# Attention: products with V issued in four groups of key tiles per block, TensorE in order of emission, one combination per query tile

## The chip, the cores and the metric

One core of a Trainium2 chip. The metric is the device time of one execution in microseconds (us), lower is better. Engines are named TensorE (PE), VectorE (DVE), ScalarE (ACT), GpSimd (POOL) and SyncE (SP, which issues the DMAs).

## The reference

A backbone of two layers over 256 context tokens and 2048 latent tokens, 1024 features. Each layer projects the normed stream, runs four branches side by side and projects their outputs back. The change lies in the branches A (differential attention) and B (grouped-query attention), which have four heads each, and are computed together, head by head:

```
# A: two softmax maps per head, q and k of 32 features, v of 64
s = jnp.einsum('bqhmd,bkhmd->bhmqk', q, k).astype(jnp.float32) * (DA_QK ** -0.5)
p = jax.nn.softmax(s, axis=-1)
w = p[:, :, 0] - lam * p[:, :, 1]
o = jnp.einsum('bhqk,bkhd->bqhd', w.astype(v.dtype), v)
# B: four query heads of 64 on two heads of k and v
s = jnp.einsum('bqhgd,bkhd->bhgqk', q, k).astype(jnp.float32) * (GQ_HD ** -0.5)
p = jax.nn.softmax(s, axis=-1)
return jnp.einsum('bhgqk,bkhd->bqhgd', p.astype(v.dtype), v)
```

Latent queries read all 2304 keys; context queries (in the first layer alone) read the 256 context keys.

## The kernel before

`attention` (line 743) runs once per layer, between the input projections and the output projection. It goes over the four heads, and within a head over eight **blocks** of 256 latent queries (two query tiles of 128), in the first layer with a small block of context queries ahead. That makes 32 full blocks a layer and 64 in all. A full block (`block`, line 825) has these steps:

- `da_chunk` (line 835), 12 times: for query tile qt, map m and one third of the keys (768), two TensorE matmuls of 384 columns write scores into a PSUM tile `s`; one VectorE scan (line 850) copies them to SBUF as `e` and keeps a running minimum of the negated scores.
- `da_exp` (line 856), 4 times: one ScalarE Exp over 2304 keys (line 858), with the sum of the row.
- `da_comb` (line 860), two parts per query tile: the two maps are combined, E0 + E1 r, where r comes from the sums (lines 865 and 866). The first 512 keys are done by ScalarE (line 871) and GpSimd (line 872), the other 1792 by VectorE in two instructions of 896 (line 875).
- `g_chunk` (line 880), 6 times: scores of B into a tile `s` of the same PSUM pool, and a VectorE scan (line 888) for their maximum alone. The pool `pf` has two such tiles, for `da_chunk` and `g_chunk` together.
- `qb` (line 894), twice: the maximum is transposed and written into the operand `qb`.
- `tr` (line 900), 9 times: four TensorE transposes (line 905) turn the combined map of two key tiles, and ScalarE copies them to SBUF as `wt` (line 909).
- `gs` (line 911), 9 times: scores of B, already turned (lines 917 and 918), their Exp by ScalarE as `gp` (line 920), and their sum over key tiles by GpSimd as `acc` (line 926).
- `pvm` (line 931), 18 times, one per key tile: the products with V. One matmul writes rows 64 to 127 of the PSUM tile `pv` (B, from `gp`), the other rows 0 to 63 (A, from `wt`); each uses half of the array's columns, and their records show them side by side. [...]
- `o1`, `o2`, `o3` (lines 942 to 970): `pv` is copied, transposed back, divided by the sums (four VectorE instructions at line 964) and stored.

The order comes from `Slots` (line 52): each step is put at a slot number with a priority, and the steps are traced in that order. The blocks overlap: a block's scores take its slots 0 to 17, its transposes, turned scores and products with V the 18 slots behind them, in which the next block's scores run. The lines that place the products are these:

```
S.at(b0 + 2 * u, lambda u=u: tr(u), 1)
S.at(b0 + 2 * u + 1, lambda u=u: gs(u), 4)
for j in range(2):
    S.at(b0 + 2 * u + 5.5 + j, lambda u=u, j=j: pvm(u, j), 5)
```

The traced program then goes through a scheduler, which sets the final order of each engine and may move an instruction ahead of others. Every engine executes its own list in that order.

Of the kernel before, what the change touches and what calls it, by code (L numbers as in the profile page):

```python
# [9 lines left out]
F32 = mybir.dt.float32  # L10
# [3 lines left out]
AF = mybir.ActivationFunctionType  # L14
# [6 lines left out]
P = 128  # L21
# [12 lines left out]
# columns of the input projection  # L34
# [6 lines left out]
def bc(ap, dims):  # L41
    """The access pattern with its free dimensions replaced (stride 0 repeats)."""
    return bass.AP(tensor=ap.tensor, offset=ap.offset, ap=[list(ap.ap[0])] + [list(d) for d in dims])


def rows_bc(ap, n):
    """A row of DRAM repeated over n partitions."""
# [4 lines left out]
class Slots:  # L52
    """Emission in the order of slots, so that blocks overlap."""
# [18 lines left out]
class Kernel:  # L72
# [3 lines left out]
    # ---------------------------------------------------------------- helpers  # L76
    def split_weights(self, wh, wl, src, w, col=None, stage=None):
        """wh + wl = src (scaled per row where col is given), both float32r."""
# [20 lines left out]
    def mm3(self, ps, hh, hl, wh, wl, c0, c1, ks=range(KT)):  # L99
        """ps = (hh + hl)^T (wh + wl) to float32's accuracy, over row tiles ks of KT."""  # L100
# [6 lines left out]
    def weights(self, wp, name, widths):  # L107
        """Tiles for the two parts of weights; the first are laid where a pool before frees its first."""
# [5 lines left out]
    def table(self):  # L114
        """The table set of Exp and Ln together."""
        return self.nc.scalar.preload_act_table_set("natural_log_exp_and_others")

    def rstd(self, pool, out, ss, n, tag, after=None):
        """out = (ss + n EPS)^(-1/2), with a step of Newton's on the engine's tables"""
# [17 lines left out]
    # ---------------------------------------------------------------- all  # L137
    def run(self):
        tc, nc, I = self.tc, self.nc, self.I
        self.table()  # L140
        with ExitStack() as cx:
# [6 lines left out]
            # per layer: (1 + sc) g and sh by feature, lambda  # L148
# [59 lines left out]
    # ---------------------------------------------------------------- modulation  # L208
    def ada(self, i, parts, wp, pp, start=False):
        """Shift (0), scale (1) and gate (2) of layer i, in steps of about a tile of weights."""  # L210
        nc, I = self.nc, self.I
        NB = 256
        if 2 in parts:
            # lambda, negated
# [11 lines left out]
        for r in parts:  # L226
# [33 lines left out]
            else:  # L260
                # rms_norm leaves out the factor 32 = sqrt(1024), which is put here
# [7 lines left out]
    # ---------------------------------------------------------------- q, k, v of A and B  # L269
    def rope(self, out, x, tmp, cos, sin, H, d):  # L270
        """out = x cos + swap(x) sin over H heads of d; x may lie in PSUM."""
# [20 lines left out]
    def pa_load(self, i, t):  # L292
        """Tile t of the stream, normed (but for gains), and its rotary factors."""
# [12 lines left out]
    def pa_front(self, i, t, xn, pt, tag):  # L306
        """Tile t modulated and transposed, in two float32r parts."""
# [19 lines left out]
    def h_tile(self, i, t):  # L327
        """The same, from memory."""
# [4 lines left out]
    def pa_weights(self, i):  # L333
        """Weights of q and k of A, and of q, k and v of B."""
# [8 lines left out]
    def proj_attn(self, i, X, H, wcx, W):  # L343
        nc, I, D = self.nc, self.I, self.D[i]
        last = i == DEPTH - 1
        with ExitStack() as cx:
# [29 lines left out]
            for t in range(NTILE):  # L376
# [10 lines left out]
                def part_a():  # L387
                    """A: q, k"""
# [950 lines left out]
```

## Time and profile before

| | |
|---|---|
| median of 3 runs | 4003.65 us (3995.14 to 4005.86) |
| span of the profiled execution, the one time that its page tells | 4001.6 us |
| TensorE busy | 3883.3 us, 97% |
| VectorE busy | 2730.4 us, 68% |
| ScalarE busy | 2322.1 us, 58% |
| GpSimd busy | 1461.5 us, 37% |
| attention, first layer, first to last score matmul | about 665 to 1601 us of the span |
| attention, second layer | about 2660 to 3567 us |

The shares of the page are means over the whole span. Attention is read by windows of its own: in the steady part of a layer one block follows the other at a fixed distance. Matmul records overlap, since matmuls are pipelined, so the distance between their starts tells more than their durations. In the chain of waits a run of equal matmuls is one row with its share of the time. On VectorE an instruction's record overlaps the next one's by some 0.08 us.

### The profile page before, as it was taken

To read this page: it belongs to the slowest core of one execution; us is meant where nothing else is said; L and a number is where in the kernel's file an instruction comes from. 1 tells how busy PE (TensorE), PEld (TensorE's weight loads), DVE (VectorE), ACT (ScalarE), POOL (GpSimd) and SP (SyncE) were. 2 spreads that over 40 slices of the span, in tenths; PEclk is the share of its full clock that TensorE was granted. 3 is DMA by queue.
4 is the path that set the end of the run, shared out by engine and by line. 5 is a ranking of instruction groups with operands and counts; after the bars stand their busy time and mean duration, and the time that the engine had idled before them with its cause. 6 is when DMAs were issued, how large, how long until landed. Compare 5 with 4: busy or idle time off the path is not lost.

```text
span 4001.6 us, 67227 instructions
## 1 busy us (share of the span) xinstructions
PE 3883.3 (97%) x24276; PEld 2877.1 (72%) x24276; DVE 2730.4 (68%) x6088; ACT 2322.1 (58%) x4181; POOL 1461.5 (37%) x1454
## 2 busy tenths in 40 slices
PE   7999998999999999999999999989999999999999
PEld 5888885666666666677878888866666666667777
DVE  5555545898989889533346654468999999976443
ACT  4434444677777777634444434447777777766554
POOL 1223221555555555311111132225555555552111
PEclk9999998999999999999999999979999999999999
DMA  8444334211020100533235431141111201015321
GB/s 265 148 150 133 115 99 111 65 41 43 22 67 21 33 24 24 182 103 104 94 120 179 143 119 56 60 106 49 45 34 29 56 21 31 22 50 169 103 95 58
DMA packets 302795, 339.21 MB, mean 85 GB/s; under 512 B 99384, under 2 KB 245760, under 8 KB 302464
## 3 DMA queue, kind: packets, MB, share of 16 engines
q1 hardware_dynamic: 302464, 334.92, 27.7%
q8 instruction: 192, 3.15, 0.3%
q14 instruction: 139, 1.14, 0.1%
HBM read 234.15 MB, written 100.62 MB: 84 GB/s over the span
## 4 chain that ended last, share of the span: by engine, by line
PE 87%; DMA 4%; DVE 4%; issue 2%; ACT 2%; POOL 1%; SPq 1%; DVEq 0%; POOLq 0%; ACTq 0%
PE pv L937 16%; PE s L845 8%; PE b L905 7%; PE b L917 5%; PE s L883 4%; PE b L918 3%; PE pz L103 3%; PE po L103 3%; PE po L105 3%; PE pz L105 3%; PE pz L104 3%; PE po L104 3%; PE pc L103 2%; PE pc L105 2%; PE pc L104 2%
## 5 line engine op out<-in xcount | busy, mean ns | idle before, releaser
L926 POOL TENSOR_TENSOR acc<-acc,gp 128x512 f32<-128x512 f32 x448 | 711.2, 1587 | 465.4 <-ACT gp L920 455.6
L937 PE MATMUL pv<-gp,v 128*64 128x256 f32 x2320 | 709.6, 400 | 0.0
L937 PE MATMUL pv<-wt,v 128*64 128x256 f32 x2320 | 709.2, 400 | 0.0
L858 ACT ACTIVATE e<-e,dm 128x2304 f32<-128x2304 f32 x256 | 568.7, 2221 | 48.3 <-DVE e L850 48.3
L850 DVE TENSOR_SCALAR_CACHE_REDUCE e<-s,dm 128x768 f32<-128x768 f32 x512 | 509.3, 1012 | 97.4 <-PE s L845 96.6
L845 PE MATMUL s<-dak,daq 128*128 128x384 f32 (+1 forms) x1568 | 461.8, 377 | 17.4 <-DMA daq<-aqk 7.4
L875 DVE SCALAR_TENSOR_TENSOR e<-e,r 128x896 f32<-128x896 f32 x256 | 457.8, 1808 | 0.1
L920 ACT ACTIVATE gp<-b 128x512 f32<-128x512 f32 x580 | 345.7, 596 | 100.5 <-PE b L918 87.9
L909 ACT COPY wt<-b 128x512 f32<-128x512 f32 x580 | 338.5, 585 | 112.5 <-PE b L905 99.0
L937 PEld LDWEIGHTS pv<-gp,v 128*64 128x64 f32 x2320 | 236.8, 135 | 205.8 <-issue 142.6
L905 PE MATMUL b<-ident,e 128*128 128x128 f32 x2304 | 360.7, 278 | 1.2 <-POOL e L872 1.2
L917 PE MATMUL b<-qa,ka 128*128 128x256 f32 x1160 | 354.2, 321 | 0.2
L905 PEld LDWEIGHTS b<-ident,e 128*128 128x128 f32 x2304 | 269.6, 141 | 93.7 <-issue 53.9
L845 PEld LDWEIGHTS s<-dak,daq 128*128 128x128 f32 x1568 | 247.7, 197 | 106.0 <-issue 85.5
L918 PE MATMUL b<-qb,kb 128*128 128x256 f32 x1160 | 305.5, 281 | 0.0
L917 PEld LDWEIGHTS b<-qa,ka 128*128 128x128 f32 x1160 | 220.7, 190 | 97.2 <-issue 71.6
L872 POOL TENSOR_TENSOR e<-e 128x512 f32<-128x512 f32 x128 | 171.2, 1337 | 306.5 <-ACT e L871 306.2
L888 DVE TENSOR_SCALAR_CACHE_REDUCE junk<-s,gm 128x768 bf16<-128x768 f32 x256 | 259.6, 1014 | 31.3 <-PE s L883 21.0
L850 DVE TENSOR_SCALAR_CACHE_REDUCE e<-s 128x768 f32<-128x768 f32 x256 | 239.6, 952 | 49.1 <-PE s L845 48.9
L1195 POOL TENSOR_TENSOR x<-x,g 128x512 f32<-128x512 f32 x66 | 88.8, 1345 | 427.1 <-DVE g L1193 406.4
L937 PEld LDWEIGHTS pv<-wt,v 128*64 128x64 f32 x2320 | 237.0, 135 | 0.6 <-issue 0.3
L883 PE MATMUL s<-ka,qa 128*128 128x384 f32 (+1 forms) x784 | 227.6, 373 | 9.1 <-DVE junk L888 6.2
(289 smaller groups left out, 9127.5 us busy)
## 6 DMA issues: line engine op xcount, KB each, us to landing
hT<-hT SPq DMA_DIRECT2D x104, 512.0 KB
dak<-aqk SPq DMA_DIRECT2D x96, 192.0 KB
daq<-aqk SPq DMA_DIRECT2D x136, 128.0 KB
wst<-in_w_in_dram SPq DMA_DIRECT2D x64, 256.0 KB
xa<-in_ada_w_dram SPq DMA_DIRECT2D x32, 512.0 KB
bst<-bst SPq DMA_DIRECT2D x68, 194.0 KB
xa<-xb SPq DMA_DIRECT2D x19, 512.0 KB
v<-v SPq DMA_DIRECT2D x16, 576.0 KB
```

Source lines behind the costliest of these rows:

```text
L845: nc.tensor.matmul(s[:, u, :hc], lhsT=Q["daq"][m][:, qt * P : (qt + 1) * P], rhs=R["dak"][m][c][:, u * hc : (u + 1) * hc], start=True, sto ...
L850: nc.vector.tensor_scalar(out=E[qt, m][:, c * ch : (c + 1) * ch].rearrange("p (u f) -> p u f", u=2), in0=s[:, :, :hc], scalar1=-SC, scalar ...
L858: nc.scalar.activation(e, e, AF.Exp, bias=NM[qt, m], scale=-1.0, accum_out=L[qt][:, m : m + 1])
L875: nc.vector.scalar_tensor_tensor(out=E0[:, a : a + w], in0=E1[:, a : a + w], scalar=RR[qt][:, 2:3], in1=E0[:, a : a + w], op0=ALU.mult, op ...
L883: nc.tensor.matmul(s[:, u, :hc], lhsT=Q["QA"][:, qt * P : (qt + 1) * P], rhs=R["KA"][c][:, u * hc : (u + 1) * hc], start=True, stop=True,)
L905: nc.tensor.transpose(s[:, j * 256 + qt * P : j * 256 + (qt + 1) * P], W[qt][:, k * P : (k + 1) * P], ident)
L909: nc.scalar.copy(WT[u], s)
L917: nc.tensor.matmul(o, lhsT=R["KA"][k // 6][:, ks], rhs=Q["QA"], start=True, stop=False)
L918: nc.tensor.matmul(o, lhsT=R["KB"][k // 6][:, ks], rhs=Q["QB"], start=False, stop=True)
L920: nc.scalar.activation(g, s, AF.Exp, scale=0.125)
L926: nc.gpsimd.tensor_tensor(out=B["acc"], in0=B["acc"], in1=g, op=ALU.add)
L937: nc.tensor.matmul(B["pv"][o : o + 64, :256], lhsT=R["V"][:, k, o : o + 64], rhs=x[:, js], start=k == 0, stop=k == nkt - 1,)
```

## The change

All of it lies in `attention`. The lines shift by three to five in the changed kernel.

```diff
+            cx.enter_context(self.tc.manual_schedule(engines={PE}))
...
                         if m == 0:
                             L[qt] = sp.tile([P, 2], F32, name="l", tag="l", bufs=6)
+                            if qt == 0:
+                                B["r"] = sp.tile([P, 2, 4], F32, name="r", tag="r", bufs=4)
...
-                        r = RR[qt] = sp.tile([P, 4], F32, name="r", tag="r", bufs=6)
-                        nc.vector.reciprocal(r[:, 0:2], l)
+                        r = RR[qt] = B["r"][:, qt]
+                        nc.vector.reciprocal(r[:, 0:3:2], l)
...
-                    rl = sp.tile([P, 4], F32, name="rl", tag="rl", bufs=3)
-                    nc.vector.reciprocal(rl, op[:, 256:260])
-                    B["op"], B["rl"] = op, rl
+                    nc.vector.reciprocal(B["r"][:, :, 1], op[:, 256:260:2])
+                    B["op"] = op
...
-                    for qt in range(2):
-                        for o, sc in ((0, RR[qt][:, 0:1]), (64, rl[:, 2 * qt : 2 * qt + 1])):
-                            dst, src = ob[:, qt, o : o + 64], op[:, qt * P + o : qt * P + o + 64]
-                            nc.vector.tensor_scalar(out=dst, in0=src, scalar1=sc, scalar2=None, op0=ALU.mult)
+                    nc.vector.tensor_tensor(
+                        out=ob.rearrange("p t (b d) -> p t b d", d=64),
+                        in0=B["op"][:, 0:256].rearrange("p (t b d) -> p t b d", t=2, d=64),
+                        in1=bc(B["r"][:, :, 0:2], [[4, 2], [1, 2], [0, 64]]), op=ALU.mult,
+                    )
...
-                    npt = 2 if full else 1
+                    npt = 1
...
-                    S.at(s, lambda qt=qt: qb(qt), 2)
+                    S.at(s + full, lambda qt=qt: qb(qt), 8 if full else 2)
...
-                        for j in range(2):
-                            S.at(b0 + 2 * u + 5.5 + j, lambda u=u, j=j: pvm(u, j), 5)
-                    e = b0 + 2 * (nu - 1) + 6.5
+                    for us in ((0, 1), (2, 3), (4, 5), (6, 7, 8)):
+                        for u in us:
+                            for j in range(2):
+                                S.at(b0 + 2 * us[-1] + 5.5, lambda u=u, j=j: pvm(u, j), 5)
+                    e = b0 + 2 * (nu - 1) + 5.5
```

So: TensorE's list in attention is the traced order, without the scheduler (`manual_schedule`). The 18 products with V of a block are traced in four runs, of 4, 4, 4 and 6. The VectorE part of a combination is one instruction of 1792 keys per query tile. The division at the end of a block is one instruction with the factors of both branches in one tile `r`. The transposes of `qb` come a slot later.

What TensorE has around a long run of products, in a steady block. Before (`s` are score tiles, `pv` the products with V, `b` with `e` the transposes, `b` with `qa` and `qb` the turned scores):

```order
L937 MATMUL pv<-gp,v 64x256
L937 MATMUL pv<-wt,v 64x256
L845 MATMUL s<-dak_32776,daq_33068 128x384 x2
L905 MATMUL b<-ident,e 128x128 x4
L845 MATMUL s<-dak_32779,daq_33066 128x384 x2
L937 MATMUL pv<-gp,v 64x256
L937 MATMUL pv<-wt,v 64x256
L917 MATMUL b<-qa,ka 128x256
L918 MATMUL b<-qb,kb 128x256
```

The run of six of the changed kernel, of whose twelve rows the first and the last two stand here:

```order
L909 MATMUL b<-ident,e 128x128 x4
L848 MATMUL s<-dak_32513,daq_32718 128x384 x2
L921 MATMUL b<-qa,ka 128x256
L922 MATMUL b<-qb,kb 128x256
L848 MATMUL s<-dak_32516,daq_32720 128x384 x2
L941 MATMUL pv<-gp,v 64x256
L941 MATMUL pv<-wt,v 64x256
...
L909 MATMUL b<-ident,e 128x128 x4
L848 MATMUL s<-dak_32432,daq_32718 128x384 x2
```

Products that stood singly between score tiles stand in one run, between the score tile of one slot and the transposes of the next. A steady block had 15 runs of products, and has 4; in the whole program they go from 976 to 264.

A run of four between score tiles of B (line 887), in the changed kernel, where again the first two of eight rows stand for the run:

```order
L887 MATMUL s<-ka,qa 128x384 x2
L921 MATMUL b<-qa,ka 128x256
L922 MATMUL b<-qb,kb 128x256
L941 MATMUL pv<-gp,v 64x256
L941 MATMUL pv<-wt,v 64x256
...
L887 MATMUL s<-ka,qa 128x384 x2
L909 MATMUL b<-ident,e 128x128 x4
```

Here a run lies between two score tiles, behind a pair of turned scores. The other two runs of four stand ahead of transposes: one right behind the transposes of `o2`, one behind the last score tile of B.

VectorE in a steady block before, from the division on (`ob`), with the scans of scores (`e`, `junk`) and the halves of the combination (L875):

```order
L964 TENSOR_SCALAR ob<-b,rl 128x64
L865 RECIPROCAL r<-l 128x2
L850 TENSOR_SCALAR e,dm<-s,dm 128x768
L866 SCALAR_TENSOR_TENSOR r<-l,nlam_70,r 128x1
L888 TENSOR_SCALAR junk,gm<-s 128x768
L875 SCALAR_TENSOR_TENSOR e<-e,r 128x896 x2
L888 TENSOR_SCALAR junk,gm<-s 128x768
L888 TENSOR_SCALAR junk,gm<-s,gm 128x768
```

The same place now:

```order
L958 RECIPROCAL r<-b 128x2
L879 SCALAR_TENSOR_TENSOR e<-e,r 128x1792
L963 TENSOR_TENSOR ob<-b,r 128x256
L853 TENSOR_SCALAR e,dm<-s,dm 128x768 x2
L892 TENSOR_SCALAR junk,gm<-s 128x768 x2
L892 TENSOR_SCALAR junk,gm<-s,gm 128x768 x2
L869 RECIPROCAL r<-l 128x2
```

One instruction of 1792 stands where two of 896 were, and two score tiles of A are queued behind it; the block's second combination stands behind the last scan of B.

## Rows read from the trace of the kernel before

**Rows 1.** The page's part 1: busy us, share of the span, instructions.

```profile
PE 3883.3 (97%) x24276; PEld 2877.1 (72%) x24276; DVE 2730.4 (68%) x6088; ACT 2322.1 (58%) x4181; POOL 1461.5 (37%) x1454
```

**Rows 2.** Windows, eight steady blocks: length, busy of PE, PEld, DVE, ACT, POOL, clock, DMA.

```profile
2902.80:3129.40 226.60, 225.72 (x1506) 150.97 (x1505) 205.82 (x392) 166.17 (x249) 127.90 (x89) 1.00 0.16 40
```

**Rows 3.** Waits in the same eight blocks: us in total, times, longest.

```profile
DVE e L850 <- PE s L845: 15.6, 40, 0.5
PEld b L896 <- PE pv L937: 4.3, 8, 0.5
DVE junk L888 <- PE s L883: 3.8, 16, 0.3
```

**Rows 4.** Chain of waits, two steady blocks: start, us, what, number of matmuls.

```profile
2909.38 0.58 PE pv L937 x4
2909.97 0.59 PE b L905 x4
...
2913.32 1.01 PE pv L937 x8
...
2917.34 1.47 PE pv L937 x12
...
2925.66 0.36 PE s L845 x2
2926.25 0.58 PE pv L937 x4
2926.83 0.56 PE s L845 x2
2927.39 0.44 PE b L905 x4
...
2941.65 1.01 PE pv L937 x8
```

**Rows 5.** Timeline of PE, four turned scores and the score tile behind them.

```profile
1202.65 0.28 PE L918 MATMUL b<-qb,kb 128*128 128x256 f32 x1
1202.77 0.29 PE L917 MATMUL b<-qa,ka 128*128 128x256 f32 x1
1202.89 0.28 PE L918 MATMUL b<-qb,kb 128*128 128x256 f32 x1
1203.01 0.51 PE L845 MATMUL s<-dak,daq 128*128 128x384 f32 x2
```

**Rows 6.** Timeline of DVE in one steady block.

```profile
2904.05 0.25 DVE L964 TENSOR_SCALAR ob<-b,r 128x64 f32<-128x64 f32 x1
2904.22 0.27 DVE L964 TENSOR_SCALAR ob<-b,rl 128x64 f32<-128x64 f32 x1
2904.41 0.28 DVE L964 TENSOR_SCALAR ob<-b,r 128x64 f32<-128x64 f32 x1
...
2907.13 4.26 DVE L875 SCALAR_TENSOR_TENSOR e<-e,r 128x896 f32<-128x896 f32 x2
...
2915.86 1.95 DVE L875 SCALAR_TENSOR_TENSOR e<-e,r 128x896 f32<-128x896 f32 x1
...
2918.68 1.22 DVE L875 SCALAR_TENSOR_TENSOR e<-e,r 128x896 f32<-128x896 f32 x1
...
2921.57 1.01 DVE L850 TENSOR_SCALAR_CACHE_REDUCE e<-s,dm 128x768 f32<-128x768 f32 x1
2922.51 0.08 DVE L850 DVE_READ_ACCUMULATOR e<-s,dm 128x1 f32 x1
2922.51 1.01 DVE L850 TENSOR_SCALAR_CACHE_REDUCE e<-s,dm 128x768 f32<-128x768 f32 x1
```

**Rows 7.** Timeline of POOL in the same block.

```profile
2907.07 1.29 POOL L872 TENSOR_TENSOR e<-e 128x512 f32<-128x512 f32 x1 [2.48 <-ACT e L871]
2908.32 5.57 POOL L926 TENSOR_TENSOR acc<-acc,gp 128x512 f32<-128x512 f32 x3
2915.59 1.27 POOL L872 TENSOR_TENSOR e<-e 128x512 f32<-128x512 f32 x1 [1.71 <-ACT e L871]
2916.83 2.12 POOL L926 TENSOR_TENSOR acc<-acc,gp 128x512 f32<-128x512 f32 x1
2920.51 1.29 POOL L926 TENSOR_TENSOR acc<-acc,gp 128x512 f32<-128x512 f32 x1 [1.57 <-ACT gp L920]
```

**Rows 8.** Groups by line and shape in the eight blocks, DVE: busy us, mean ns, idle before.

```profile
L875 DVE SCALAR_TENSOR_TENSOR e<-e,r 128x896 f32<-128x896 f32 x32 | 59.4, 1875 | 0.0
```

More of the change, by code (lines that the diff above doesn't have):

```diff
@@ L863, in da_comb @@
                     if part == 0:
-                        r = RR[qt] = sp.tile([P, 4], F32, name="r", tag="r", bufs=6)
-                        nc.vector.reciprocal(r[:, 0:2], l)
+                        r = RR[qt] = B["r"][:, qt]
+                        nc.vector.reciprocal(r[:, 0:3:2], l)
                         nc.vector.scalar_tensor_tensor(
-                            out=r[:, 2:3], in0=l[:, 0:1], scalar=nlam, in1=r[:, 1:2], op0=ALU.mult, op1=ALU.mult
+                            out=r[:, 3:4], in0=l[:, 0:1], scalar=nlam, in1=r[:, 2:3], op0=ALU.mult, op1=ALU.mult
                         )
@@ L870, in da_comb @@
                         if npl:
-                            nc.scalar.activation(E1[:, :npl], E1[:, :npl], AF.Copy, scale=r[:, 2:3])
+                            nc.scalar.activation(E1[:, :npl], E1[:, :npl], AF.Copy, scale=r[:, 3:4])
                             nc.gpsimd.tensor_tensor(out=E0[:, :npl], in0=E0[:, :npl], in1=E1[:, :npl], op=ALU.add)
@@ L875, in da_comb @@
                     nc.vector.scalar_tensor_tensor(
-                        out=E0[:, a : a + w], in0=E1[:, a : a + w], scalar=RR[qt][:, 2:3], in1=E0[:, a : a + w],
+                        out=E0[:, a : a + w], in0=E1[:, a : a + w], scalar=RR[qt][:, 3:4], in1=E0[:, a : a + w],
                         op0=ALU.mult, op1=ALU.add,
@@ L953, in o2 @@
                         )
-                    rl = sp.tile([P, 4], F32, name="rl", tag="rl", bufs=3)
-                    nc.vector.reciprocal(rl, op[:, 256:260])
-                    B["op"], B["rl"] = op, rl
+                    nc.vector.reciprocal(B["r"][:, :, 1], op[:, 256:260:2])
+                    B["op"] = op
                 def o3():
-                    op, rl = B["op"], B["rl"]
                     ob = sp.tile([P, 2, P], F32, name="ob", tag="ob", bufs=3)
-                    for qt in range(2):
-                        for o, sc in ((0, RR[qt][:, 0:1]), (64, rl[:, 2 * qt : 2 * qt + 1])):
-                            dst, src = ob[:, qt, o : o + 64], op[:, qt * P + o : qt * P + o + 64]
-                            nc.vector.tensor_scalar(out=dst, in0=src, scalar1=sc, scalar2=None, op0=ALU.mult)
+                    nc.vector.tensor_tensor(
[3 more added lines that the diff above has]
+                    )
                     for o in (0, 64):
```

## The prediction

> **What bounds the kernel now.** I read the shares first: TensorE is busy 97% of the span, VectorE 68% [rows 1]. That is a mean over stages, so I went to the windows of attention. Eight steady blocks take 226.60 us, 28.33 each; two equal runs of the chain, one block apart, stand 28.33 us apart as well (2913.32 and 2941.65) [rows 2, 4]. In them TensorE is busy 225.72 us (28.2 a block) at the full clock, VectorE 205.82 (25.73 a block), ScalarE 166.17, GpSimd 127.90 [rows 2]. So TensorE bounds the stage, and VectorE has only 2.6 us a block to spare. The waits agree: VectorE waits for score tiles, 15.6 and 3.8 us in eight blocks, never over 0.5 us at once, and TensorE's only wait of size is 0.5 us a block for the transposes of the maximum, most of it hidden behind the products' tail [rows 3].
>
> What does TensorE spend on the products with V? In the chain a run of one call (four records) has 0.58 us, of two 1.01, of three 1.47 [rows 4]. A further call costs 0.43 to 0.46, so the run itself costs 0.14. Its neighbours pay too: a score tile beside runs has 0.56 where one behind other work has 0.36, and the transposes behind a run have 0.59 instead of 0.44 [rows 4]. **A run costs 0.14 + 0.15 to 0.20, some 0.31 us, beside its products.** There are 15 runs in a steady block.
>
> **The change, part by part.**
>
> *Fewer runs.* 15 become 4: 11 x 0.31 = 3.4 us a block off TensorE. Its work falls from 28.2 to 24.8 us, under VectorE's 25.7. The 18 products themselves stay. So from here on TensorE alone no longer sets the block, and the question is what VectorE does, and how well the two fit.
>
> *The combination in one piece.* The four halves of a block took 2.13 twice (4.26 together), 1.95 and 1.22 us [rows 6], 59.4 / 8 = 7.43 a block [rows 8]. The same instruction is short when GpSimd is idle (1.22; GpSimd's add overlapped only its first 0.27 us) and nearly twice as long beside a GpSimd addition (2.13, under rows 2907.07 and 2908.32 of GpSimd) [rows 6, 7]. Per element that is 1.36 against 2.38 ns. One instruction of 1792 is therefore bounded by about 2.1 us (alone: two of 1.22, less the overlap and one start-up) and 4.26 (beside GpSimd throughout). GpSimd's own work is unchanged, 127.90 / 8 = 16.0 us a block [rows 2], and the 512 keys that it does itself start within 0.3 us of the VectorE part, with queued additions to `acc` behind them, up to 6.8 us on end [rows 7]. So I take 3.75 each, the mean of the halves before, nearest to the long end: 7.5 a block, no gain beyond one start-up.
>
> *The division.* Four instructions of 64 columns, 0.17 to 0.19 us from start to start [rows 6], become one of 256 that reads PSUM. Bounds: 0.19 (no more than one of 64) and 0.76 (all four). A scan of 768 columns from PSUM needs 0.94 [rows 6], so 256 come to about 0.4: 0.36 saved.
>
> *VectorE's work* is then 25.73 - 7.43 + 7.5 - 0.36 = 25.4 us a block.
>
> *VectorE's new waits.* TensorE may be ahead by two score tiles only (the pool `pf`), and executes its list in order. Around the run of six it goes: score tile, six products, four transposes, score tile. From one tile's end to the next's that is 0.58 + 5 x 0.445 = 2.80, then 0.59, then 0.36: 3.75 us [rows 4]. Meanwhile VectorE has the finished tile (0.94) and at most what is left of the one before: that one must have been begun when TensorE began the new tile, so at most 0.94 - 0.36 = 0.58. It idles 3.75 - 1.52 = 2.2 us at least, 2.8 at most: 2.4. Around the run of four between two tiles of B: turned scores 4 x 0.12 = 0.48 [rows 5], the run 0.58 + 3 x 0.445 = 1.92, a tile between runs 0.56: 2.96. Less 1.52 or 0.94: 1.4 to 2.0, taken as 1.6. The other two runs of four stand where VectorE is inside a combination (3.75 against 1.92 + 0.59), and cost it nothing. Idle in sum: 4.0 us a block (3.6 to 4.8).
>
> *Why it can't catch up.* Each combination holds both score tiles. The tile of TensorE's list that is third from its start waits for the combination, the division and a scan; from `o2` on TensorE has 1.92 + 0.59 + 0.36 + 0.48 + 0.36 = 3.7 us of work until then, VectorE needs 0.1 + 3.75 + 0.4 + 0.94 = 5.2. TensorE stalls about 1.5 us there, and likewise at the second combination, and whatever it saved on runs goes there. Before, the list let it do single products in these places.
>
> *The rest.* The transposes of `qb` a slot later remove the small wait [rows 3]; TensorE's stalls hide that, so 0. The tile `r` and the end `e` change no instruction on the path. SP issues the same loads and stores in each block, and TensorE's list outside attention is the same: 0.
>
> **Sum.** A block takes VectorE's work and idle time: 25.4 + 4.0 = 29.4 us, against 28.33: +1.07. TensorE's 24.8 plus its stalls fit in that. With 64 full blocks this is +68 us. The profiled span is 4001.6 us, and no time of that execution around it is told; the median of the runs is 4003.65, 2 us more. On the median: **4072 us**, 1.7% slower. Bounds: combinations of 3.3 with idle time of 3.6 give 24.5 + 3.6 = 28.1 (-15 us); of 4.26 with 4.2, 26.4 + 4.2 = 30.6 (+147, all at the bad end).
>
> **Rivals.** A difference under 0.3% (12 us, 0.19 us a block) is about what a measurement of this kernel can't tell from none.
>
> 1. *VectorE at its floor (faster).* If VectorE is fed without gaps, a block falls to its work, 25.4 us: 2.93 x 64 = 188 us less, 3816. Half of the idle time gone gives 27.4: 60 us less, 3944. It decides at 2.9 us of idle time a block; below that the kernel is faster. For it: TensorE's saving is real in every row of a run, and VectorE is 91% busy already. Against it: two score tiles hold 1.9 us of scans, and the run of six with its transposes lasts 3.4. The Trainium skill, TensorEngine Tiling (Array Packing), section PSUM Bottleneck, says that where the array is sped up by tiling, the copies out of PSUM may become the bound. By that rule alone the block would be the work of the emptying engine, which is this rival. No row before shows it: VectorE still waits for score tiles [rows 3]. Chance 0.24, mostly between 3925 and 3990.
>
> 2. *No difference.* The longer instruction meets less of GpSimd: combinations of 3.2 each make 24.3 of work, with 4.0 idle 28.3. For it: one of the four halves ran nearly alone [rows 6, 7]. Against it: a piece twice as long is less able to miss GpSimd's queue. 4004 us, chance 0.10.
>
> 3. *The order doesn't do what it says*, as where the list were still rearranged. The list of the changed program shows the four runs, so I count this with the second.
>
> **How the numbers follow.** The forecast (slower, VectorE and TensorE by turns waiting) has 0.66, the second rival 0.10, the first 0.24. Slower by over 0.3%: 0.66; within: 0.10; faster: 0.24. The slow case by itself runs from 4016 to 4120. For 8 in 10 the range must take in the slow case almost whole, the second rival and the near part of the first: 3925 to 4118.
>
> **What would show it.** After: (a) distance of two blocks 29.4 us; 28.33 or less refutes me. (b) TensorE's runs with 16 and 24 records, about 1.9 and 2.8 us, and its busy time near 25 us a block; if it stays at 28, the cost of a run was misread. (c) VectorE waiting for TensorE in pieces of over 1.4 us, twice a block, 3.6 to 4.8 us in sum. (d) TensorE waiting for the scans at lines 853 and 892, 1 to 2 us twice a block, where before it waited for none. (e) The combination at 3.5 to 4.2 us each. (f) The division near 0.4. If (e) comes out near 2, the kernel is faster and the step that failed is the price beside GpSimd; if (c) is under 2.9, it is the two-tile argument.

## The result, and the profile after

The changed kernel takes **4034.64 us** (median of 4 runs, 4030.99 to 4040.03), the kernel before 4001.32 (median of 4, 3995.14 to 4005.86). The ratio is 1.0082, with a 95% interval of 1.0067 to 1.0096: slower by 33 us. I had said slower by 68. The sign held, and the time lies in my range; the size was twice too large, and the sign held in part by luck, as the account of the sum below works out.

Lines of the changed kernel: scans of A's scores L853, of B's L892, the combination L879 (its GpSimd share L876, its two small instructions L869 and L870), additions to `acc` L928 to L933, products with V L941, division L963.

Part 1 of the page, to compare with [rows 1]:

```profile
PE 3758.6 (93%) x24276; PEld 2967.0 (74%) x24276; DVE 2613.1 (65%) x5756; ACT 2328.6 (58%) x4181; POOL 1526.7 (38%) x1454
```

TensorE was busy 125 us less and VectorE 117 us less, and the whole took longer: both now wait for each other. Eight steady blocks, with the columns of [rows 2]:

```profile
2926.20:3154.40 228.20, 208.32 (x1506) 160.42 (x1505) 189.39 (x352) 166.92 (x249) 135.97 (x90) 1.00 0.15 39
```

A block takes 228.20 / 8 = 28.53 us (before 28.33), of which TensorE is busy 26.04 (28.2) and VectorE 23.67 (25.73). The waits in these blocks (total, times, longest), against [rows 3]:

```profile
DVE e L853 <- PE s L848: 23.1, 16, 2.5
...
DVE junk L892 <- PE s L887: 13.2, 8, 1.7
...
PE s L887 <- DVE e L853: 9.6, 8, 1.2
...
PE b L909 <- POOL e L876: 5.5, 8, 0.7
```

VectorE waits for scores 23.1 + 13.2 us in eight blocks, 4.5 a block in all, in pieces of up to 2.5 and 1.7. TensorE waits for a scan 1.2 us a block, and 0.7 for GpSimd's share of the combination. The chain of waits, one block, shows the new runs:

```profile
2931.64 0.62 PE s L887 x2
...
2933.67 1.88 PE pv L941 x16
...
2941.50 3.02 POOL e L876
2944.56 0.55 PE b L909 x3
...
2948.14 2.74 PE pv L941 x24
2950.88 0.59 PE b L909 x4
2951.47 0.37 PE s L848 x2
2951.85 1.03 DVE e L853 x3
```

Runs of 16 and 24 records (four to a call of `pvm`) take 1.88 and 2.74 us, and GpSimd's addition stands in the chain with 3.02 us. It took 1.27 to 1.29 before [rows 7]. The timeline of VectorE in that block, where [rows 6] showed halves:

```profile
2926.22 0.88 DVE L870 SCALAR_TENSOR_TENSOR r<-l,nlam,r 128x1 f32<-128x1 f32 x1
...
2928.04 2.28 DVE L879 SCALAR_TENSOR_TENSOR e<-e,r 128x1792 f32<-128x1792 f32 x1
2930.24 0.41 DVE L963 TENSOR_TENSOR ob<-b,r 128x256 f32<-128x256 f32 x1
2930.58 1.00 DVE L853 TENSOR_SCALAR_CACHE_REDUCE e<-s,dm 128x768 f32<-128x768 f32 x1
...
2936.13 1.02 DVE L892 TENSOR_SCALAR_CACHE_REDUCE junk<-s,gm 128x768 bf16<-128x768 f32 x1 [1.64 <-PE s L887]
...
2940.51 2.86 DVE L879 SCALAR_TENSOR_TENSOR e<-e,r 128x1792 f32<-128x1792 f32 x1
...
2951.85 0.96 DVE L853 TENSOR_SCALAR_CACHE_REDUCE e<-s 128x768 f32<-128x768 f32 x1 [2.51 <-PE s L848]
```

And that of GpSimd, where [rows 7] stood:

```profile
2925.81 2.63 POOL L930 TENSOR_TENSOR acc<-acc,gp 128x512 f32<-128x512 f32 x2 [4.60 <-ACT gp L924]
2928.39 3.05 POOL L876 TENSOR_TENSOR e<-e 128x512 f32<-128x512 f32 x1
...
2940.22 1.27 POOL L930 TENSOR_TENSOR acc<-acc,gp 128x512 f32<-128x512 f32 x1 [0.73 <-ACT gp L924]
2941.46 3.04 POOL L876 TENSOR_TENSOR e<-e 128x512 f32<-128x512 f32 x1
```

Read the two together. At 2928.04 VectorE begins its combination; GpSimd is still adding until about 2928.4. The combination waits 0.3 us, then runs 1.95. GpSimd's next addition, begun at 2928.39, ends at 2931.44, only 1.1 us after the combination: its own 1.28 begins about when the combination ends. At 2940.51 the same happens with a wait of about 1 us. And L870, one column wide, takes 0.88 us instead of some 0.2: it ends at 2927.10, about when the first of GpSimd's pair of additions does. In the groups of the eight blocks (busy us, mean ns), against [rows 8]:

```profile
L879 DVE SCALAR_TENSOR_TENSOR e<-e,r 128x1792 f32<-128x1792 f32 x16 | 41.2, 2573 | 0.0
...
L870 DVE SCALAR_TENSOR_TENSOR r<-l,nlam,r 128x1 f32<-128x1 f32 x16 | 8.7, 543 | 0.3
```

The combination costs 41.2 / 8 = 5.15 us a block. I had said 7.5.

**Where the 33 us lie.** The starts of the first transposes of `o2` in each block mark the program. Before and after, in us:

| stretch | before | after | difference |
|---|---|---|---|
| start to first mark | 719.6 | 723.2 | +3.6 |
| layer 0, first to last mark | 911.4 | 942.9 | +31.5 |
| between the layers | 1101.9 | 1088.8 | -13.1 |
| layer 1, first to last mark | 863.6 | 874.4 | +10.8 |

The rest, to the end, is 1.1 shorter; the sum is, to rounding, the 31.8 us between the two spans (4001.6 and 4033.4). Of the +3.6 ahead of the first mark, 3.5 lie ahead of the first score tile of attention (665.0 against 668.5 us), in work that the change does not touch. Steady blocks give only 0.2 us each, 13 in 64. Most of the loss lies in layer 0, beside the context blocks: the four marks' distances around the first of them are 31.6 + 33.9 + 5.6 + 27.0 = 98.1 us, before 29.7 + 27.1 + 5.2 + 29.1 = 91.1. The other two cost 6.8 and 8.8, and the last block of each layer about 5. Windows there (columns as above, clock third from the end):

```profile
894.80:926.40 31.60, 27.80 (x197) 21.95 (x196) 24.75 (x55) 19.93 (x38) 17.75 (x12) 0.95 0.37 90
926.40:960.30 33.90, 29.69 (x195) 21.61 (x193) 24.84 (x46) 21.61 (x31) 13.47 (x11) 0.90 0.19 46
...
944.00:948.00 4.00, 1.95 (x5) 1.14 (x6) 3.72 (x8) 0.16 (x1) 3.45 (x3) 0.78 0.17 49
948.00:952.00 4.00, 4.00 (x18) 2.90 (x19) 2.61 (x6) 1.06 (x3) 0.00 (x0) 0.50 0.00 0
```

TensorE is busy 1.95 of 4 us from 944 to 948, waiting for VectorE, and the granted clock then stands at 0.50, the 1.2 GHz level. Before, it was 1.00 in all these blocks.

Of the 13.1 us that come back between the layers, 9.6 lie ahead of the second layer's first score tile, some 5 of them in the input projections (298.0 us before, at a granted clock of 0.98; 292.8 after, at 1.00), and 3.5 in the layer's first block (73.2 against 69.6 us). No run takes these apart.

### The profile page after: what moved, and what is told of

It reads as the page before. It is cut to its first block, busy times and chain, and to the rows that moved or that the text cites. A ratio compares the mean times of both kernels' runs of the same rounds, so it can differ in the third digit from the quotient of the medians.

```text
span 4033.4 us, 66612 instructions
## 1 busy us (share of the span) xinstructions
PE 3758.6 (93%) x24276; PEld 2967.0 (74%) x24276; DVE 2613.1 (65%) x5756; ACT 2328.6 (58%) x4181; POOL 1526.7 (38%) x1454
## 3 DMA queue, kind: packets, MB, share of 16 engines
q1 hardware_dynamic: 302464, 334.92, 27.3%
## 4 chain that ended last, share of the span: by engine, by line
PE 64%; DVE 18%; POOL 6%; issue 5%; DMA 4%; ACT 3%; SPq 0%; DVEq 0%; POOLq 0%; ACTq 0%
PE pv L941 8%; DVE e L853 5%; DVE junk L892 4%; POOL e L876 4%; DVE e L879 4%; PE s L848 4%; PE b L909 4%; PE s L887 3%; PE pz L103 3%; PE po L103 3%; PE po L105 3%; PE po L104 3%; PE pz L105 3%; PE pz L104 3%; PE pc L103 2%
## 5 line engine op out<-in xcount | busy, mean ns | idle before, releaser
L930 POOL TENSOR_TENSOR acc<-acc,gp 128x512 f32<-128x512 f32 x448 | 588.2, 1313 | 586.3 <-ACT gp L924 580.5
L941 PE MATMUL pv<-gp,v 128*64 128x256 f32 x2320 | 560.8, 387 | 0.0
L941 PE MATMUL pv<-wt,v 128*64 128x256 f32 x2320 | 560.7, 387 | 0.0
L853 DVE TENSOR_SCALAR_CACHE_REDUCE e<-s,dm 128x768 f32<-128x768 f32 x512 | 500.4, 1011 | 57.3 <-PE s L848 57.0
L848 PE MATMUL s<-dak,daq 128*128 128x384 f32 (+1 forms) x1568 | 460.1, 377 | 33.2 <-DVE junk L892 13.2
L941 PEld LDWEIGHTS pv<-gp,v 128*64 128x64 f32 x2320 | 297.6, 137 | 169.1 <-issue 22.6
L876 POOL TENSOR_TENSOR e<-e 128x512 f32<-128x512 f32 x128 | 365.3, 2854 | 72.5 <-ACT e L875 72.5
L853 DVE TENSOR_SCALAR_CACHE_REDUCE e<-s 128x768 f32<-128x768 f32 x256 | 235.6, 951 | 159.5 <-PE s L848 158.8
L887 PE MATMUL s<-ka,qa 128*128 128x384 f32 (+1 forms) x784 | 245.0, 395 | 95.2 <-DVE e L853 77.1
L879 DVE SCALAR_TENSOR_TENSOR e<-e,r 128x1792 f32<-128x1792 f32 x128 | 330.0, 2578 | 0.3
L892 DVE TENSOR_SCALAR_CACHE_REDUCE junk<-s,gm 128x768 bf16<-128x768 f32 x256 | 260.3, 1017 | 107.6 <-PE s L887 95.9
L921 PE MATMUL b<-qa,ka 128*128 128x256 f32 x1160 | 311.4, 291 | 12.8 <-ACT wt L913 12.6
L941 PEld LDWEIGHTS pv<-wt,v 128*64 128x64 f32 x2320 | 297.6, 137 | 0.0
L1200 POOL TENSOR_TENSOR x<-x,g 128x512 f32<-128x512 f32 x66 | 88.7, 1344 | 443.9 <-DVE g L1198 423.3
L887 PEld LDWEIGHTS s<-ka,qa 128*128 128x128 f32 x784 | 120.3, 193 | 171.3 <-DVE e L853 99.1
```

Source lines behind the costliest of these rows:

```text
L848: nc.tensor.matmul(s[:, u, :hc], lhsT=Q["daq"][m][:, qt * P : (qt + 1) * P], rhs=R["dak"][m][c][:, u * hc : (u + 1) * hc], start=True, sto ...
L853: nc.vector.tensor_scalar(out=E[qt, m][:, c * ch : (c + 1) * ch].rearrange("p (u f) -> p u f", u=2), in0=s[:, :, :hc], scalar1=-SC, scalar ...
L876: nc.gpsimd.tensor_tensor(out=E0[:, :npl], in0=E0[:, :npl], in1=E1[:, :npl], op=ALU.add)
L879: nc.vector.scalar_tensor_tensor(out=E0[:, a : a + w], in0=E1[:, a : a + w], scalar=RR[qt][:, 3:4], in1=E0[:, a : a + w], op0=ALU.mult, op ...
L887: nc.tensor.matmul(s[:, u, :hc], lhsT=Q["QA"][:, qt * P : (qt + 1) * P], rhs=R["KA"][c][:, u * hc : (u + 1) * hc], start=True, stop=True,)
L892: nc.vector.tensor_scalar(out=junk[:, :ch].rearrange("p (u f) -> p u f", u=2), in0=s[:, :, :hc], scalar1=-1.0, scalar2=GM.get(qt, BIG), op ...
```

## Experiments

The theory after the result: a VectorE instruction that reads two tiles in SBUF and a GpSimd addition go **one at a time**, in order of start. The rival is the prediction's own: both go on, at a lower rate per element. Times are medians, ratios against the kernel before on the same chip.

### e1: the changed kernel, combination in halves

```diff
-                    npt = 1
+                    npt = 2 if full else 1
```

> The changed kernel, but with the combination of a full block in two halves again; all else as changed. Theory (one at a time): a VectorE instruction with two SBUF inputs and a GpSimd addition don't share time; whichever began first runs to its end at full speed and the other waits for it. Then each half takes 0.97 us and waits for at most one GpSimd addition (1.28): four halves a block cost about 7.0 us in sum where the two whole ones cost 5.15, GpSimd's addition for the combination falls from about 3.0 back to 1.3 to 1.9, and a block grows by 1.2 to 1.9 us: 4110 to 4160 us. Rival (a slowdown per element, as in the prediction's price): two halves cost what one whole instruction costs, but for 0.06 us of start-up each: 5.3 us a block, 4035 to 4050 us.

Measured: 4152.75 us, 1.0381 [1.0364, 1.0399]. The groups of eight blocks, VectorE and GpSimd:

```profile
L879 DVE SCALAR_TENSOR_TENSOR e<-e,r 128x896 f32<-128x896 f32 x32 | 57.7, 1823 | 0.0
...
L876 POOL TENSOR_TENSOR e<-e x16: 2127/2132/2157, 2925.9 to 3154.3; 128x512 f32<-128x512 f32 x16
```

(The second row gives least, median and longest ns.) The halves cost 57.7 / 8 = 7.2 us a block against 5.15 for whole ones, though the same elements are read. A second instruction pays a second wait. Only GpSimd's addition is a little longer than expected, 2.13 us. The rival falls.

A block takes 30.7 us, more than I expected, and not all of the excess is the waits. Blocks of two lengths stand among the steady ones, and the granted clock tells them apart (columns as above):

```profile
2923.64:2953.70 30.06, 26.15 (x189) 20.11 (x188) 25.57 (x47) 20.86 (x32) 16.36 (x12) 1.00 0.12 35
2953.70:2985.15 31.45, 27.57 (x190) 21.45 (x189) 25.67 (x47) 21.18 (x32) 16.32 (x12) 0.95 0.31 82
```

At the full clock the halves cost 1.5 us a block against the change, as expected; 23 blocks of the longer kind add some 30 us. So of the 118 us between this kernel and the changed one, about a quarter goes with the clock (an estimate from these two lengths).

### e2: the kernel before, combination in one piece alone

```diff
-                    npt = 2 if full else 1
+                    npt = 1
```

> The kernel before with one part of the change alone: the combination in one piece. Theory (one at a time): it waits for one GpSimd addition at most, so 2.2 to 2.7 us each, 4.4 to 5.4 a block where the halves took 7.4; VectorE's work falls by 2 us or more, but TensorE sets the pace there with 28.2 us of work, so the time changes by little: 3970 to 4005 us, with VectorE's waits for score tiles grown by what the combination gives back, and GpSimd's addition at line 872 longer (2 us or more instead of 1.3). Rival (per element, combinations of 3.75): no gain on VectorE, and TensorE waits behind each whole combination: 4010 to 4060 us.

Measured: 3997.45 us, 0.9994 [0.9985, 1.0004], no difference. Groups of eight blocks, VectorE:

```profile
L875 DVE SCALAR_TENSOR_TENSOR e<-e,r 128x1792 f32<-128x1792 f32 x16 | 42.6, 2663 | 0.0
```

5.3 us a block instead of 7.43, and GpSimd's L872 goes from 1.28 to 3.06 us. VectorE's gain goes into longer waits for TensorE, which sets that kernel's pace. This part of the change is worth nothing by itself.

### e3: the changed kernel without most additions to `acc`

```diff
                     if u == 1:
-                        nc.gpsimd.tensor_tensor(out=B["acc"], in0=GP[0], in1=g, op=ALU.add)
-                    elif u > 1:
-                        nc.gpsimd.tensor_tensor(out=B["acc"], in0=B["acc"], in1=g, op=ALU.add)
+                        nc.gpsimd.tensor_scalar(out=B["acc"], in0=g, scalar1=1.0, scalar2=1.0, op0=ALU.mult, op1=ALU.add)
```

> The changed kernel, with the additions to acc at line 930 left out (the sum of B's denominators is left out of the computation; the first addition becomes one with a constant), so that GpSimd does in a combination's neighbourhood only its own 512 columns. Theory (one at a time): the pair goes in order of start. Where GpSimd's addition begins first, the combination waits for it and takes 1.95 + 1.2 = about 3.1 us; where the combination begins first, it takes 1.95 and GpSimd's addition about 3. No combination lies between (2.3 to 2.8), the one-column instruction at line 870 takes 0.16 to 0.3 us instead of 0.54, and a block falls by 0.5 to 1 us: 3970 to 4005 us. Rival (per element): an addition of 1.2 us beside the combination lengthens it by about half of that: all of them at 2.4 to 2.7 us; the time within 15 us of the changed kernel.

Measured: 3973.09 us, 0.9931 [0.9916, 0.9946]; 27.8 us a steady block. One block on VectorE's timeline:

```profile
2935.18 0.22 DVE L870 SCALAR_TENSOR_TENSOR r<-l,nlam,r 128x1 f32<-128x1 f32 x1
...
2936.34 3.10 DVE L879 SCALAR_TENSOR_TENSOR e<-e,r 128x1792 f32<-128x1792 f32 x1
...
2949.65 2.08 DVE L879 SCALAR_TENSOR_TENSOR e<-e,r 128x1792 f32<-128x1792 f32 x1
```

and on GpSimd's:

```profile
2936.30 1.27 POOL L876 TENSOR_TENSOR e<-e 128x512 f32<-128x512 f32 x1 [6.03 <-ACT e L875]
2949.97 2.90 POOL L876 TENSOR_TENSOR e<-e 128x512 f32<-128x512 f32 x1 [12.40 <-ACT e L875]
2956.76 0.62 POOL L928 TENSOR_SCALAR acc<-gp 128x512 f32<-128x512 f32 x1 [3.89 <-ACT gp L924]
```

This is the cleanest pair of the study. GpSimd first by 0.04 us: its addition takes 1.27 and the combination 3.10. VectorE first by 0.32 us: the combination takes 2.08 and the addition 2.90. There is no combination of 2.4 to 2.7 us here, and of the 128 in the whole trace 127 take 2.06 to 2.08 or 3.08 to 3.19; one, begun 0.32 us behind an addition, takes 2.83. In order of start, one after the other: **shown**.

### e4: three runs of six calls

```diff
-                    for us in ((0, 1), (2, 3), (4, 5), (6, 7, 8)):
+                    for us in ((0, 1, 2), (3, 4, 5), (6, 7, 8)):
```

> The changed kernel with three groups of three pairs of key tiles, (0-2), (3-5), (6-8): three runs of six calls instead of runs of four, four, four, six. Theory: what the changed kernel loses is that TensorE's list and VectorE's long instructions stand badly to each other (4.5 us a block of VectorE waiting for scores, 1.5 of TensorE waiting for scans, 1 for the combination). With runs placed so that one lies beside each combination, the waits for B's score tiles (1.6 a block) go, and TensorE's wait at line 887 halves: a block of 26.3 to 27.3 us, 3895 to 3960 us. Rival (the run of six is what costs, 2.4 us of wait each, as the prediction counted it): more runs of six add a wait of 2.4 in place of the 1.6, so a block of 28.5 to 30.5: 4030 to 4150 us.

Measured: 3944.13 us, 0.9862 [0.9847, 0.9877]; 27.0 us a steady block. VectorE's waits in eight blocks:

```profile
DVE e L853 <- PE s L848: 24.1, 23, 2.6
...
DVE e L853 <- PE b L922: 3.0, 1, 3.0
```

The wait around one run of six stays (24.1, and one of 3.0 that the view puts down to turned scores, against 23.1), the wait for B's tiles (13.2) is gone, and TensorE's waits for scans fall from 9.6 to 0.9. A run beside a combination costs VectorE next to nothing (waits of 0.3 to 0.4 us at most), as the prediction argued for two of the four. Beside the context blocks the loss stays: 30.4 + 34.6 + 3.6 + 27.6 us.

### e5: TensorE kept at work beside the context blocks

```diff
+            def fill(R, n):
+                for _ in range(n):
+                    nc.tensor.matmul(
+                        PV[0][:, 256:512], lhsT=R["KA"][0][:, :P], rhs=R["KA"][0][:, :256], start=False, stop=False
+                    )
...
+                        if with_ctx and bi > 9 and bi % 9 == 1 and (qt, c) in ((1, 0), (1, 2)):
+                            S.at(s, lambda c=c: fill(R, 10 + 2 * c), -0.5)
...
+                if bi > 0 and not full:
+                    S.at(base, lambda: fill(R, 6), 6.5)
+                    S.at(s, lambda: fill(R, 10), 1.5)
```

> The changed kernel with matmuls that serve nothing (128 rows, 256 columns, into unused columns of pv's bank) ahead of the four places in which TensorE waits beside a context block of layer 0: 6 ahead of the context block's first score tile, 10 ahead of its turned maximum, 10 and 14 ahead of two tiles of B in the block behind it; 40 at each of three context blocks. Theory: some two thirds of the changed kernel's loss lies at these three places, because TensorE's waits gather there and its granted clock then falls (0.50 at 948 to 952 us) for some 8 us, in which the products take twice as long. With the waits filled the clock stays at 1.00 there and the stretch of four blocks (31.6 + 33.9 + 5.7 + 28.0 us) shrinks by 4 to 6 us, though the filling takes up to 1 us of it: 4016 to 4026 us. Rival (the order beside the context block costs by itself, the clock is a bystander): the clock stays up, the stretch does not shrink, or grows by the filling: 4033 to 4045 us.

Measured: 4025.78 us, 1.0060 [1.0048, 1.0073]. Windows of the same two blocks:

```profile
891.20:922.00 30.80, 28.75 (x214) 22.68 (x213) 24.83 (x55) 19.89 (x38) 17.83 (x12) 1.00 0.36 92
922.00:953.30 31.30, 29.59 (x218) 22.64 (x217) 24.59 (x46) 21.52 (x31) 13.41 (x11) 1.00 0.21 50
```

The granted clock is 1.00, and the stretch of four goes from 98.1 to 94.7 us. At the other two it goes from 97.9 to 96.1 and from 99.9 to 96.2; in sum that is the 8.9 us by which the medians differ. Both had a share: of some 7 us lost at each place the clock explains about 3 (1.8 to 3.7, less than the 4 to 6 expected), and the rest stays. The rival puts it down to the waits themselves; that is what is left, and no run takes it apart.

### e6: the three runs moved

```diff
-                    for us in ((0, 1), (2, 3), (4, 5), (6, 7, 8)):
+                    for us, d in (((0, 1, 2), 4.5), ((3, 4, 5), 4.5), ((6, 7, 8), 6.5)):
...
-                                S.at(b0 + 2 * us[-1] + 5.5, lambda u=u, j=j: pvm(u, j), 5)
-                    e = b0 + 2 * (nu - 1) + 5.5
+                                S.at(b0 + 2 * us[-1] + d, lambda u=u, j=j: pvm(u, j), 5)
+                    e = b0 + 2 * (nu - 1) + 6.5
```

> The changed kernel with three runs of six calls, the first two one slot earlier and the last one slot later than the groups of e4_three_runs stood. Theory: TensorE's work with few runs is well under 25.5 us a block and VectorE's is 23.2, so what is left over is only how the places of the runs fit VectorE's long instructions; an event-by-event replay of this order, with durations of the changed kernel's trace and GpSimd's and VectorE's two-input instructions one at a time, gives 25.4 us a block where it gives 28.3 for the changed kernel and 26.4 for e4_three_runs (measured 28.5 and 27.0): 25.6 to 26.4 us a block, 3850 to 3900 us. Rival (a run of six costs its wait of 2.4 us wherever it stands, so that the number of runs of six sets the time): no better than e4_three_runs: 3935 to 3960 us.

Measured: 3899.19 us, 0.9747 [0.9732, 0.9762]. Eight steady blocks:

```profile
2892.20:3103.40 211.20, 205.74 (x1507) 162.26 (x1505) 180.12 (x353) 164.57 (x250) 122.45 (x90) 1.00 0.16 43
```

26.4 us a block, at the end of the range. TensorE is busy 25.7 of them, so it sets the pace again, at 0.9 us over the work that the prediction's first step gave it (24.8), and that with one run fewer. With the same 18 products and three runs of six, where they stand is worth 0.6 us a block against e4. The rival falls.

### e7: the changed kernel with TensorE's list left to the scheduler

```diff
-            cx.enter_context(self.tc.manual_schedule(engines={PE}))
             junk = kp.tile([P, CH], BF16, name="junk", tag="junk", bufs=1)
```

> The changed kernel without one part: TensorE's list is left to the scheduler again, as before the change, while groups, combination and division are as changed. Theory: the four groups stay (they come from the slots), but the scheduler moves score tiles and transposes between them by its own clock, which eases the two waits of VectorE a little: the replay gives 28.2 us a block against 28.3, and no added wait beside the context blocks, where the changed kernel loses some 8 us each time: 4000 to 4025 us. Rival (the order of emission is what makes the groups work, the rearranged list breaks them up again): runs of 2, 4 and 8 records come back, and the block goes to 29 us or more: over 4050 us.

Measured: 4009.69 us, 1.0029 [1.0018, 1.0039]; 28.6 us a steady block. My time came true for a wrong reason. The list of this kernel has 13 runs of products in these blocks: the scheduler does take the groups apart, as the rival said, and TensorE is busy 98% of the time (224.28 of 228.90 us in eight blocks). The rival's time, over 4050, is wrong as well. Steady blocks are as long as in the changed kernel. The 25 us between the two kernels lie elsewhere: in the profiled executions 23 lie beside the three context blocks, at the first of them 28.1 + 29.3 + 6.6 + 27.0 = 91.0 us here, where the clock stays at 1.00, and 6 at the layers' last blocks; some of it is given back between the layers.

### e8: e6, with whole slots in the context block

```diff
-                            s += 1 if full else 0.5
+                            s += 1 if full else 1
...
-                        s += 1 if full else 0.5
+                        s += 1 if full else 1
```

> e6_moved, and the context block's score tiles a whole slot apart instead of half a slot (six slots instead of three), so that the full blocks beside it keep their distance. Theory: in e6_moved the block beside each context block takes 33.4 us instead of 26.4, because two combinations come together there, TensorE waits for them, and then runs at 0.50 of its clock for some 8 us. With whole slots the replay (which knows no clock) takes the long block from 30.5 to 27.5 us and the context block from 2.3 to 6.3; if TensorE's waits no longer gather, the clock stays up and the stretch of four blocks (28.8 + 33.4 + 2.6 + 27.3 = 92.1 us) falls to 86 to 89, three times over: 3882 to 3895 us. Rival (the extra slots only move the wait into the context block): 92 us or more, 3897 to 3910 us.

Measured: **3892.83 us**, 0.9730 [0.9715, 0.9744], the fastest kernel here, 2.7% under the kernel before. The stretch at the first context block is 27.0 + 27.7 + 6.8 + 27.2 = 88.7 us (92.1 in e6), with the clock at 1.00. At the second one it is at 0.89 in one block of 29.9, so the cure is not complete.

### e9: the groups alone, on the kernel before

```diff
-                        for j in range(2):
-                            S.at(b0 + 2 * u + 5.5 + j, lambda u=u, j=j: pvm(u, j), 5)
-                    e = b0 + 2 * (nu - 1) + 6.5
+                    for us in ((0, 1), (2, 3), (4, 5), (6, 7, 8)):
+                        for u in us:
+                            for j in range(2):
+                                S.at(b0 + 2 * us[-1] + 5.5, lambda u=u, j=j: pvm(u, j), 5)
+                    e = b0 + 2 * (nu - 1) + 5.5
```

> The kernel before with one part of the change alone: products with V in the four groups, with TensorE's list left to the scheduler, the combination in halves and the division in four. The list then has 10.8 runs a block instead of 15, as the scheduler takes groups apart. Theory: TensorE sets the pace of the kernel before, a run costs it 0.31 us beside its products, so 4.2 runs fewer take 1.3 us off a block, as long as VectorE's 25.7 us of work fit: 27.0 to 27.5 us a block (the replay gives 27.15), 3925 to 3965 us. Rival (runs cost TensorE nothing that its queue does not hide, or VectorE's halves behind GpSimd bound the block): within 15 us of the kernel before.

Measured: 3951.72 us, 0.9873 [0.9858, 0.9887]. Eight steady blocks:

```profile
2903.50:3122.20 218.70, 214.18 (x1506) 155.09 (x1504) 201.09 (x392) 164.26 (x249) 122.58 (x89) 1.00 0.16 42
```

27.3 us a block. In these blocks 10 runs are left of 15, and TensorE's work falls from 28.2 to 26.8: 0.29 us a run, where the prediction had 0.31. But that is no fixed price. In most blocks of this kernel's first layer 12 runs are left (10.8 is the mean over both layers), and there TensorE's work falls by 0.27 us for three runs fewer, a third of that price:

```profile
1064.00:1092.15 28.15, 27.94 (x190) 19.32 (x188) 24.77 (x49) 20.45 (x32) 15.71 (x12) 1.00 0.08 22
```

That fewer runs are less work for TensorE and a shorter block is **shown**, 50 us in all. What one run costs is not: 0.09 to 0.29 us in this kernel, and what the difference hangs on stays open.

### e10: the order of emission alone, on the kernel before

```diff
+            cx.enter_context(self.tc.manual_schedule(engines={PE}))
             junk = kp.tile([P, CH], BF16, name="junk", tag="junk", bufs=1)
```

> The kernel before with one part of the change alone: TensorE in order of emission in attention, with the products still single (18 runs a block), halves and four divisions as before. Theory: the scheduler's list was fitted to VectorE's long instructions; in order of emission TensorE has 18 runs (0.9 us more work) and waits for scans behind each half: 30.5 to 32 us a block (the replay gives 31.6), 4140 to 4240 us. So the order by itself loses some 3 us a block, and the groups win back most of it. Rival (TensorE stays at work throughout, as in the kernel before, whatever the list): 29.1 us a block for the three more runs, 4040 to 4060 us.

Measured: 4223.04 us, 1.0551 [1.0533, 1.0568]; 32.1 us a block, again of two lengths: 31.5 us at the full clock and, in 21 blocks, 33.0 at a lower one, which makes some 30 of the 221 us. Waits in eight blocks:

```profile
DVE e L851 <- PE s L846: 54.5, 80, 1.6
...
PE b L897 <- DVE junk L889: 14.2, 8, 1.8
```

VectorE waits for A's tiles 6.8 us a block. TensorE waits not behind the halves, as I had expected, but 1.8 us a block at the transposes of `qb`, which want the last maximum of B. The change puts these a slot later.

The parts side by side, in us a steady block of the second layer (where the runs are counted) and in all:

| kernel | runs a block | block | time |
|---|---|---|---|
| before | 15 | 28.3 | 4001 |
| one-piece combination alone (e2) | 14 | 28.0 | 3997 |
| groups alone (e9) | 10 | 27.3 | 3952 |
| order of emission alone (e10) | 18 | 32.1 | 4223 |
| all but the order (e7) | 13 | 28.6 | 4010 |
| all but the one-piece combination (e1) | 4 | 30.7 | 4153 |
| the change | 4 | 28.5 | 4035 |
| three runs (e4) | 3 | 27.0 | 3944 |
| three runs, moved (e6) | 3 | 26.4 | 3899 |

So the effects don't add. The order of emission costs 221 us by itself. The one-piece combination gains nothing alone and 118 us within that order (from e1). The groups gain 50 us alone, and some 70 within it (from e10 to e1, a step that holds the division and the later transposes of `qb` as well). Those two were not run alone.

## Why the prediction was right in sign and wrong in size

- **Runs.** Right in length: 1.88 and 2.74 us against 1.92 and 2.80. The price of 0.31 us a run is nearly right in e9's second layer (0.29), but it is not the same everywhere: here 11 runs fewer took 2.2 us a block off TensorE's busy time, not 3.4, which is 0.20 a run. As TensorE did not set the pace, the sum did not feel it.
- **The combination in one piece: the step that failed.** It read "So I take 3.75 each, the mean of the halves before, nearest to the long end: 7.5 a block, no gain beyond one start-up". It measured 2.57 each, 5.15 a block. I had read the halves' durations as a rate, 2.38 ns an element beside GpSimd for the upper bound, and 3.75 us is 2.1 ns an element. But what stood in those durations were waits, each for one addition of GpSimd, and in the rows such a wait does not grow with the elements behind it: a whole costs 5.15 a block, halves 7.2 (e1). The rows that I used say so, if GpSimd's ends are worked out beside VectorE's [rows 6, 7]. L872 begins at 2907.07 and ends at 2908.36; the first half, issued at 2907.13, then needs 0.95 (as the third, which ends at 2917.81, 0.95 behind the end of L872 at 2916.86) and ends at 2909.3. The first L926, begun at 2908.32, runs 1.2 behind it, to 2910.5. The second half needs 0.95 from there, to 2911.4 or 2911.5; by its row it ends at 2907.13 + 4.26 = 2911.39. Two more additions of 1.2 end at 2913.9, which is 2908.32 + 5.57. The Trainium skill, SBUF — State Buffer, section Who interferes with whom, states this rule: a VectorE instruction with two SBUF inputs contends with a GpSimd instruction that reads SBUF, the first to issue holds the shared ports for its whole instruction, and issue order decides who blocks. The traces agree, e3 most plainly. Had I weighed that page of the Trainium skill, my estimate would have been about 2.0 plus at most one addition of 1.28 (its duration in the eight blocks before).
- **What else the same rule did**, and the prediction lacked. L870 has two SBUF inputs as well, and its one column takes 0.54 us in the mean instead of some 0.2: +0.66 a block. And GpSimd's own addition is now the loser: 3.05 us instead of 1.28. TensorE's transposes wait 0.7 us a block for it.
- **The division.** Right: 0.34 us from start to start against 0.4.
- **VectorE's work** came to 23.67 us, not 25.4: 2.35 less for the combination, 0.66 more for L870.
- **VectorE's new waits.** Right in place and nearly in size: 2.51 around the run of six (2.4), 1.65 between B's tiles (1.6). What I lacked is a wait of 0.37 behind the transposes that GpSimd's late addition holds up, and 0.3 in small pieces. All idle time is 28.53 - 23.67 = 4.86 us, where I had 4.0.
- **TensorE's stall.** The first is there (1.2 us, for the scans at L853), the second is the one for GpSimd.
- **The sum, and the luck in its sign.** A block takes 28.53 us, not 29.4: 0.9 us less, 55 us in 64 blocks, and 68 would have become 13. With the combination at its 5.15 and the rest as I had it, my sum gives 23.05 + 4.0 = 27.1 us a block, some 80 us faster; with L870's 0.66 as well 27.7, still 40 us faster. That the kernel is slower at all comes from 0.86 us of idle time that I lacked and from what was nowhere in my sum: I multiplied the steady block by 64 and took the blocks beside the context blocks and at a layer's end to be alike. There TensorE's waits gather, the clock falls, and some 7 us are lost three times, 5 twice; e5 shows the clock's share, about 9 us. 13 come back between the layers, and why was not tried and stays open.
- **The rivals.** The first needed under 2.9 us of idle time and found 4.86. The second had the nearer price, as combinations are short, but with 4.0 us of idle time, and its reason, that the longer instruction meets less of GpSimd, is not what the traces show. By my own sign (e) combinations near 2 us would have meant a faster kernel; at 2.57 it was still slower. That the order takes effect is shown by e7, which lacks it and has 13 runs.

## What to carry to other kernels

When an instruction is longer beside another engine's work, ask first whether it runs slowly or waits: lay the starts and ends of both engines side by side. If it waits, the price is at most one instruction of the other engine for each of its own, whatever its length, so few long ones are cheap for the waiter, but then the other engine's work becomes late, and someone waits for that. When the order of a queue is fixed by hand, the place of the long pieces against the other engine's long instructions can be worth as much as their number (45 us from e4 to e6 at three runs each, 50 us in e9 for fewer runs), and places that break the rhythm need to be costed by themselves. Look at the granted clock there, and in two blocks that should be equal: a kernel that leaves TensorE waiting can lose by the clock as well (e1, e5, e10).

## What was not expected of the hardware

- VectorE's instruction with two SBUF inputs and GpSimd's addition go strictly one after the other: 3.10 and 1.27 us, or 2.08 and 2.90, by 0.04 or 0.32 us of difference in start (e3). The waiting counts as busy time on the page of the profile. Even a single column waits its turn (0.88 us, against 0.22 alone).
- Scans that read PSUM are not touched by this: they take 0.94 to 1.02 us with an addition of GpSimd beside them and without, before and after the change.
- On GpSimd a multiplication and addition of constants on 512 columns takes 0.62 us, an addition of two tiles 1.27 (e3).
- TensorE busy 1.95 of 4 us was followed by a stretch at the 1.2 GHz level, at which it worked through a run of products; matmuls that serve nothing kept it at 1.00 and made the kernel 9 us faster (e5).
